# A hybrid transformer layer in float32: other feed-forward parts, a block-product end, and buffers in another order

## The chip, the cores and the metric

The kernel runs on one core of a Trainium2 chip. Five engines work side by side, each through its own queue in order: TensorE (PE; its weight loads are PEld), VectorE (DVE), ScalarE (ACT), GpSimd (POOL) and SyncE (SP), which issues the transfers between the chip's main memory (HBM) and the on-chip memory (SBUF). [...] The metric is the device time of one execution in microseconds (us); lower is better.

## The reference

One layer (`DEPTH` is 1) over 256 tokens of width 2048, all in float32. The mixer has 16 heads in two groups; then comes a feed-forward with a causal convolution of width 3 over the tokens.

```python
D_MODEL = 2048; SEQ = 256
D_FF = ((8 * D_MODEL // 3 + 255) // 256) * 256        # 5632 = 44 tiles of 128

def hybrid_mixer(h, ...):
    proj = h @ w_in_l
    ...                                               # q, k, v of both groups, forget gates
    out_a = forgetting_attention(qa, ka, va, c)       # softmax with a cumulative log-forget bias
    out_b = stick_breaking_attention(qb, kb, vb)      # sigmoid breaks, strictly causal
    merged = concat([rms_norm(out_a, g_fox), rms_norm(out_b, g_sb)])
    return merged @ w_out_l

def conv_ffn(h, w_up_l, conv_w_l, conv_b_l, w_down_l):
    u = h @ w_up_l                                    # 2048 -> 2 x 5632
    u = causal_depthwise_conv(u, conv_w_l) + conv_b_l
    gate, val = jnp.split(u, 2, axis=-1)
    return (jax.nn.silu(gate) * val) @ w_down_l       # 5632 -> 2048

x = x + hybrid_mixer(rms_norm(x, attn_norm), ...)
x = x + conv_ffn(rms_norm(x, ffn_norm), ...)
```

## The kernel before

**Precision.** Every matrix product is made of three: both operands are split into a high part, rounded to the format in which TensorE is fast, and a low part, the rest. `split` does that for weights: ScalarE casts the raw tile to `w_hi` (L208), VectorE subtracts to `w_lo` (L209). The products are hi x hi, hi x lo and lo x hi. Each weight tile is 1 MB, loaded by `load` (L201) through SyncE into `w_raw`, then split, then used.

**Mixer.** `token_major` (L237 to L239) and `feature_major` (L252, L257) stream weight tiles against `hT`, the normalised tokens transposed. The attention heads are generators that are stepped between the products. The last products are with `w_out`; each of their four column blocks adds to `x` (L561), sums squares for the second norm (L163, tile `junk`) and is transposed into `hT` (L148, L153, L154). All buffers of this stage lie in pools that are closed at its end: `wpool` with 3 raw, 2 hi and 2 lo tiles, `at` with what lives long (among it `oT`, the heads' outputs), `tmp` with what lives short (among it `raw` and `junk`).

**Feed-forward.** Its weights have a pool `wff` of their own (4 raw, 3 hi, 3 lo, one `w_sum`), placed where the mixer's pools were. The 44 feature tiles are taken in parts (`FFN_PARTS`): 8, 8, 8, 8, 8 and 4. Within a part, each two tiles need a `gate` and a `val` up-projection, each a `feature_major` of two halves (one weight tile, 32 matmuls each). `convolved` takes the sum out of PSUM (tile `t`, L268, L269), scales it (`up`, L597) and convolves (L601, L606). Then `silu(gate) * val` (L765, L766) is split into `g` (L768, L769). `combinations` makes from the tiles of two pairs the token sums `s` (L645 to L651), which the block products need; its `t` tiles come from the same two buffers as those of the evacuation.

**Down-projection, one part behind.** The part's down-projection runs beside the next part's up-projection: `step`, called after each half, adds `pace` to a counter, and each 16 releases one step of the generators in `behind`. For parts of 8 tiles these are `down_in_seven`: two by two blocks (two blocks of 4 feature tiles, two token tiles, 1024 columns) done in seven block products instead of eight, by sums of weights and sums of tokens. Each product is 12 matmuls of 512 columns (L675) against one split tile; between them VectorE sums weights into `w_sum` (L698, L706, L726) or a raw tile (L717) and adds the bank to `x` (L682). Its order before: w11 with `g`, then four products with token sums `s`, then w21 with `g` (the last two pairs), and a last one with `g`. Three PSUM banks are used in turn, `bank_a`, `bank_b` and `bank_c`. `down_plain` does the same columns with eight tiles' worth of plain products (L747 to L749), 24 matmuls a step. The last part of 4 tiles has its own loop of `token_major` (L783 on) with an add (L788) and the stores (L790) after each 512 columns.

**Order.** The framework lays instructions on the engines' queues by priority, which is the order of the program except where `tc.high_priority(offset=...)` moves instructions ahead: weight loads and splits by `AHEAD` = 200 instructions, PSUM evacuations by twice that. A tile that reuses a buffer waits until the last reader of the old tile is done, and a pool that is placed over closed pools waits for them.

Of the kernel before, what the change touches and what calls it, by code (L numbers as in the profile page):

```python
# [38 lines left out]
WINDOW = 2  # L39
FFN_PARTS = [(f, min(f + 8, NFT)) for f in range(0, NFT, 8)]  # L40


@with_exitstack
def hybrid_layer(
# [114 lines left out]
    def sums_of_squares(ss, c):  # L159

        for t in range(NT):
            junk = tmp.tile([P, 512], F32, name="junk", tag="raw", bufs=4)
            act.activation(junk, xt[t][:, c * 512 : (c + 1) * 512], AF.Square, accum_out=ss[:, t, c : c + 1])  # L163
# [34 lines left out]
    def load(src, into=None):  # L198
        raw = into if into is not None else wpool.tile([P, 2048], F32, name="w_raw", tag="w_raw")
        a, b = src.shape[1:]  # L200
        nc.sync.dma_start(raw[:, : a * b].rearrange("p (a b) -> p a b", a=a), src)  # L201
        return raw

    def split(raw, a, b):
        hi = wpool.tile([P, 2048], F32R, name="w_hi", tag="w_hi", bufs=n_split)
        lo = wpool.tile([P, 2048], F32R, name="w_lo", tag="w_lo", bufs=n_split)
        n = a * b
        act.copy(hi[:, :n], raw[:, :n])  # L208
# [63 lines left out]
    with ExitStack() as actx:  # L272
        n_split = 2
        wpool = actx.enter_context(tc.tile_pool(name="wpool", bufs=3))
        at = actx.enter_context(tc.tile_pool(name="at", bufs=1))
        pss = actx.enter_context(tc.tile_pool(name="pss", bufs=2, space=bass.MemoryType.PSUM))
        tmp = actx.enter_context(tc.tile_pool(name="tmp", bufs=2))

        def project(c0, cols, **kw):
# [12 lines left out]
        def fox_rows(acc, dst, g):  # L292

            rows = []
            for t in range(NT):
                raw = tmp.tile([P, 512], F32, name="raw", tag="raw", bufs=4)
                scaled(raw, acc[:, t, :], t)
                rows.append(raw)
            for t in range(NT):
                raw = rows[t]  # L300
                r3 = raw.rearrange("p (h d) -> p h d", h=4)
                sq = tmp.tile([P, 512], F32, name="sq", tag="raw", bufs=4)
                dve.tensor_tensor(sq, raw, raw, op=ALU.mult)
# [15 lines left out]
        ssq = [at.tile([P, S], F32, name=f"ssq{i}") for i in range(2)]  # L319

# [28 lines left out]
        acc_q0 = project(0, 512, pieces=(2,) * 8, before=opening)  # L349
        masks = tmp.tile([P, 4 * P], F32, name="masks", tag="raw", bufs=4)  # L350
        load_parameters(masks)
# [303 lines left out]

    def down_in_seven(f0, pairs, sums, c0):
# [4 lines left out]
        x11, x12 = xt[0][:, c0 : c0 + 512], xt[0][:, c0 + 512 : c0 + 1024]  # L661
        x21, x22 = xt[1][:, c0 : c0 + 512], xt[1][:, c0 + 512 : c0 + 1024]

        def of_pairs(h, t):
            return lambda a, part, j: pairs[2 * h + a][:, part, j, t * P : (t + 1) * P]
# [13 lines left out]

        def add(to, bank, op=ALU.add):  # L680
# [8 lines left out]
        with ahead():  # L689
            w = wpool.tile([P, 2048], F32, name="w_sum", tag="w_sum", bufs=1)  # L690
# [9 lines left out]
        product(bank_b, True, of_sums(0), parts)  # L700
        add(x22, bank_b)
        yield
# [4 lines left out]
        product(bank_b, False, of_sums(2), parts)  # L707
        add(x12, bank_b)
# [4 lines left out]
        add(x12, bank_a, ALU.subtract)  # L713
        yield
# [4 lines left out]
        product(bank_a, False, of_sums(3), parts)  # L719
        add(x22, bank_a, ALU.subtract)  # L720
# [12 lines left out]
        add(x21, bank_a)  # L733
        yield

    def down_plain(f0, pairs, c0, cols):
        for c in range(c0, c0 + cols, 512):
            acc = [psf.tile([P, 512], F32, name="bank_a", tag="a") for _ in range(NT)]
            for k0 in range(0, 2 * len(pairs), 4):
# [10 lines left out]
                if last:  # L750
                    for t in range(NT):
                        xs = xt[t][:, c : c + 512]
                        dve.tensor_tensor(xs, acc[t], xs, op=ALU.add)
                yield

    for n_part, (f_lo, f_hi) in enumerate(FFN_PARTS):
        pairs, gates, sums = [], [], []
        n_behind = 0
        last_part = n_part == len(FFN_PARTS) - 1

        pace = (11 if last_part else 14) * 8 // (f_hi - f_lo)
        for f in range(f_lo, f_hi, 2):
# [11 lines left out]
        while behind:  # L774
            n_behind, pace = 16, 0
            step()
        if not last_part:
            behind.append(down_in_seven(f_lo, pairs, sums, 0))
            if f_hi + 8 > NFT:
                behind.append(down_plain(f_lo, pairs, 1024, 1024))  # L780
            else:
                behind.append(down_in_seven(f_lo, pairs, sums, 1024))
    for c in range(4):  # L783
        acc = token_major(
            lambda k: pairs[k // 2][:, :, k % 2, :], wd, f_lo, f_hi - f_lo, 512 * c, 512
        )
        xs = x2[:, :, c * 512 : (c + 1) * 512]
        dve.tensor_tensor(xs, acc, xs, op=ALU.add)  # L788
        for t in range(NT):
            nc.sync.dma_start(of[t * P : (t + 1) * P, c * 512 : (c + 1) * 512], xs[:, t, :])  # L790

# [56 lines left out]
```

## Time and profile before

| | |
|---|---|
| time, median of 3 | 1193.19 us (1192.18 to 1194.01) |
| the profiled execution | 1194.88 us |
| its span, first to last instruction | 1193.1 us |
| TensorE busy | 1144.6 us, 96% of the span |
| TensorE weight load | 970.8 us, 81% |
| VectorE busy | 904.9 us, 76% |
| ScalarE busy | 616.8 us, 52% |
| granted TensorE clock, mean | 0.974 |
| moved from and to HBM | 229 MB, 192 GB/s over the span |
| mixer, to its last matmul | 0 to 413 us |
| feed-forward | 413 to 1193 us |

The busy share is an average over stages. In the mixer VectorE and ScalarE are about half busy; in the feed-forward parts VectorE is nine tenths busy beside a TensorE that is nearly always busy. A busy TensorE can still be slow: the granted clock says at which share of full speed it ran. "Idle before, <-" names what an engine waited for last.

### The profile page before, as it was taken

To read this page: it belongs to the slowest core of one execution; us is meant where nothing else is said; L and a number is where in the kernel's file an instruction comes from. 1 tells how busy PE (TensorE), PEld (TensorE's weight loads), DVE (VectorE), ACT (ScalarE), POOL (GpSimd) and SP (SyncE) were. 2 spreads that over 40 slices of the span, in tenths; PEclk is the share of its full clock that TensorE was granted. 3 is DMA by queue.
4 is the path that set the end of the run, shared out by engine and by line. 5 is a ranking of instruction groups with operands and counts; after the bars stand their busy time and mean duration, and the time that the engine had idled before them with its cause. 6 is when DMAs were issued, how large, how long until landed. Compare 5 with 4: busy or idle time off the path is not lost.

```text
span 1193.1 us, 14521 instructions
## 1 busy us (share of the span) xinstructions
PE 1144.6 (96%) x5894; PEld 970.8 (81%) x5894; DVE 904.9 (76%) x978; ACT 616.8 (52%) x667; POOL 0.2 (0%) x4
## 2 busy tenths in 40 slices
PE   7999999999999899997999899998999979998998
PEld 6998888888888778886888678886888868886886
DVE  4646656565565666788899989998899989999864
ACT  4644454445654545554656445554655545554641
POOL 0000000000000000000000000000000000000000
PEclk9999999999999989998999989998999989998999
DMA  6665555555445296554768556774767657665651
GB/s 224 212 218 182 173 175 173 156 166 167 151 142 176 72 324 201 184 177 151 237 213 256 187 190 212 235 238 161 242 204 234 205 174 231 219 220 176 212 176 71
DMA packets 172046, 230.27 MB, mean 193 GB/s; under 512 B 4025, under 2 KB 117835, under 8 KB 171979
## 3 DMA queue, kind: packets, MB, share of 16 engines
q1 hardware_dynamic: 171978, 229.35, 59.3%
q8 instruction: 46, 0.75, 0.3%
q14 instruction: 22, 0.17, 0.0%
HBM read 227.23 MB, written 2.10 MB: 192 GB/s over the span
## 4 chain that ended last, share of the span: by engine, by line
PE 90%; DVE 4%; ACT 3%; DMA 2%; issue 1%; SPq 0%; ACTq 0%; DVEq 0%
PE pu L252 31%; PE pu L257 15%; PE bank_a L675 8%; PE acc L238 8%; PE acc L237 8%; PE acc L239 8%; PE bank_b L675 5%; ACT w_hi L208 2%; DVE w_lo L209 2%; PE bank_c L675 2%; PE bank_a L747 1%; PE bank_a L749 1%; PE bank_a L748 1%; PE ps_x L148 1%; DMA x<-in_x_dram 0%
## 5 line engine op out<-in xcount | busy, mean ns | idle before, releaser
L209 DVE TENSOR_TENSOR w_lo<-w_raw,w_hi 128x2048 fp32r<-128x2048 f32 (+2 forms) x195 | 429.7, 2203 | 184.0 <-ACT w_hi L208 183.5
L208 ACT CAST w_hi<-w_raw 128x2048 fp32r<-128x2048 f32 (+2 forms) x195 | 358.6, 1840 | 339.0 <-PE pu L252 116.8
L252 PE MATMUL pu<-hT,w_hi 128*128 128x512 f32 x1664 | 527.5, 398 | 0.4 <-ACT w_hi L208 0.4
L257 PEld LDWEIGHTS pu<-hT,w_lo 128*128 128x128 f32 x1664 | 314.8, 189 | 76.0 <-DVE w_lo L209 1.8
L257 PE MATMUL pu<-hT,w_lo 128*128 128x256 f32 x1664 | 330.2, 280 | 1.1 <-DVE w_lo L209 1.1
L252 PEld LDWEIGHTS pu<-hT,w_hi 128*128 128x128 f32 x1664 | 261.0, 190 | 6.9 <-ACT w_hi L208 0.7
L237 PE MATMUL acc<-w_hi,hT 128*128 128x512 f32 (+1 forms) x320 | 120.4, 376 | 0.0
L238 PE MATMUL acc<-w_lo,hT 128*128 128x512 f32 (+1 forms) x320 | 119.2, 373 | 0.6 <-DVE w_lo L209 0.6
L239 PE MATMUL acc<-w_hi,hT 128*128 128x512 f32 (+1 forms) x320 | 119.0, 372 | 0.0
L208 ACT CAST w_hi<-w_sum 128x2048 fp32r<-128x2048 f32 x36 | 68.7, 1909 | 68.7 <-PE pu L252 46.5
L209 DVE TENSOR_TENSOR w_lo<-w_sum,w_hi 128x2048 fp32r<-128x2048 f32 x36 | 82.3, 2287 | 14.0 <-ACT w_hi L208 14.0
L675 PE MATMUL bank_b<-w_hi,s 128*128 128x512 f32 x144 | 58.7, 466 | 17.2 <-ACT s L650 10.3
L238 PEld LDWEIGHTS acc<-w_lo,hT 128*128 128x128 f32 x320 | 60.6, 189 | 9.7 <-DVE w_lo L209 1.5
L239 PEld LDWEIGHTS acc<-w_hi,hT 128*128 128x128 f32 x320 | 60.6, 189 | 8.8
L237 PEld LDWEIGHTS acc<-w_hi,hT 128*128 128x128 f32 x320 | 60.8, 190 | 8.1
L675 PE MATMUL bank_a<-w_hi,s 128*128 128x512 f32 x144 | 51.6, 418 | 9.8 <-ACT w_hi L208 9.8
L675 PEld LDWEIGHTS bank_b<-w_hi,s 128*128 128x128 f32 x144 | 31.9, 226 | 27.9 <-ACT s L650 11.8
L675 PE MATMUL bank_a<-w_hi,g 128*128 128x512 f32 x144 | 48.1, 395 | 0.0
L675 PEld LDWEIGHTS bank_a<-w_hi,s 128*128 128x128 f32 x144 | 28.4, 197 | 18.7 <-ACT w_hi L208 12.8
L606 DVE SCALAR_TENSOR_TENSOR gate<-up,ccol,gate 128x256 f32<-128x256 f32 x88 | 38.6, 481 | 3.6 <-ACT gate L601 3.4
L606 DVE SCALAR_TENSOR_TENSOR val<-up,ccol,val 128x256 f32<-128x256 f32 x88 | 38.2, 480 | 0.9 <-ACT val L601 0.7
L237 PE MATMUL acc<-w_hi,oT 128*128 128x512 f32 x96 | 38.1, 397 | 0.0
(186 smaller groups left out, 1182.3 us busy)
## 6 DMA issues: line engine op xcount, KB each, us to landing
w_raw<-in_w_up_dram SPq DMA_DIRECT2D x88, 1024.0 KB, 5.2
w_raw<-in_w_down_dram SPq DMA_DIRECT2D x53, 1024.0 KB, 5.1
w_raw<-in_w_in_dram SPq DMA_DIRECT2D x36, 1024.0 KB, 5.1
w_raw<-in_w_out_dram SPq DMA_DIRECT2D x16, 1024.0 KB, 5.1
w_sum<-in_w_down_dram SPq DMA_DIRECT2D x9, 1024.0 KB, 5.2
w_raw<-in_w_in_dram SPq DMA_DIRECT2D x12, 688.0 KB, 4.0
w_raw<-in_w_in_dram SPq DMA_DIRECT2D x8, 512.0 KB, 3.9
out_dram<-x SPq DMA_DIRECT2D x8, 256.0 KB, 2.5
```

Of the source, the lines that this page charges most:

```text
L148: nc.tensor.transpose(ps[:, j, t * P : (t + 1) * P], xt[t][:, (k + j) * P : (k + j + 1) * P], ident)
L208: act.copy(hi[:, :n], raw[:, :n])
L209: dve.tensor_tensor(lo[:, :n], raw[:, :n], f32(hi[:, :n]), op=ALU.subtract)
L237: nc.tensor.matmul(o, lhi, hi[:, i, :], start=first, stop=False)
L238: nc.tensor.matmul(o, lhi, lo[:, i, :], start=False, stop=False)
L239: nc.tensor.matmul(o, llo, hi[:, i, :], start=False, stop=last)
L252: nc.tensor.matmul(acc[:, j, :], hi[:, i, j * P : (j + 1) * P], hT[:, k].rearrange("p a b -> p (a b)"), start=k == 0, stop=False,)
L257: nc.tensor.matmul(acc[:, j, S:], lo[:, i, j * P : (j + 1) * P], hT[:, k, 0, :], start=False, stop=k == KT - 1,)
L606: dve.scalar_tensor_tensor(a[:, j, :], u[:, j, w : w + S], ccol[:, w, f : f + 1], a[:, j, :], op0=ALU.mult, op1=ALU.add,)
L675: nc.tensor.matmul(bank, lhs(a, l, j), r[:, i, :], start=first and i + n == 0, stop=i == 3 and n == 2, skip_group_check=not first,)
L747: nc.tensor.matmul(acc[t], g[:, 0, ts], hi[:, i, :], start=first, stop=False)
L748: nc.tensor.matmul(acc[t], g[:, 0, ts], lo[:, i, :], start=False, stop=False)
```

## The change

- The feed-forward's parts become 4, 8, 8, 8, 8, 8 tiles. The first part's down-projection is plain (`down_plain` over all 2048 columns, four steps, released at a pace of 4), those of the following four parts are two `down_in_seven` each.
- The last part has 8 tiles and its down-projection runs after all up-projections: the first 1024 columns by `down_in_seven` (called `heavy`), the other 1024 by `down_plain` (`light`), their steps interleaved by hand. Each block of 512 columns is stored as soon as its last addition is made.
- In `down_in_seven` the product of w21 with the last two pairs' `g` moves from sixth to second place, so that the products with token sums begin with the third. w21 is loaded a second time for the sum of the last product.
- Pools: raw, hi and lo weight tiles and `w_sum` get pools of their own in both stages, in another order; the mixer's `raw`, `junk`, `sq`, `masks`, `oT` and `ssq` go to a pool `late` behind the others. Counts of buffers stay as they were.

```diff
-FFN_PARTS = [(f, min(f + 8, NFT)) for f in range(0, NFT, 8)]
+FFN_PARTS = [(max(f, 0), f + 8) for f in range(-4, NFT - 4, 8)]
...
     with ExitStack() as actx:
-        n_split = 2
-        wpool = actx.enter_context(tc.tile_pool(name="wpool", bufs=3))
         at = actx.enter_context(tc.tile_pool(name="at", bufs=1))
...
         tmp = actx.enter_context(tc.tile_pool(name="tmp", bufs=2))
+        wraw = actx.enter_context(tc.tile_pool(name="wraw", bufs=3))
+        whi = actx.enter_context(tc.tile_pool(name="whi", bufs=2))
+        wlo = actx.enter_context(tc.tile_pool(name="wlo", bufs=2))
+        late = actx.enter_context(tc.tile_pool(name="late", bufs=1))
...
-        oT = [at.tile([P, 2, S], F32R, name=f"oT{h}") for h in range(2 * NH - 4)]
+        oT = [late.tile([P, 2, S], F32R, name=f"oT{h}") for h in range(2 * NH - 4)]
...
-    n_split = 3
-    wpool = ctx.enter_context(tc.tile_pool(name="wff", bufs=4))
+    wlo = ctx.enter_context(tc.tile_pool(name="wlo2", bufs=3))
+    whi = ctx.enter_context(tc.tile_pool(name="whi2", bufs=3))
+    wraw = ctx.enter_context(tc.tile_pool(name="wraw2", bufs=4))
+    wsum = ctx.enter_context(tc.tile_pool(name="wsum", bufs=1))
...
+        adds = {}
+
+        def add(t, half, bank, op=ALU.add):
+            c = c0 + 512 * half
+            to = xt[t][:, c : c + 512]
             with tc.high_priority(offset=2 * AHEAD):
                 dve.tensor_tensor(to, to, bank, op=op)
+            adds[t, half] = adds.get((t, half), 0) + 1
+            if final and adds[t, half] == (1 if (t, half) == (1, 0) else 2):
+                store(t, c)
...
         product(bank_a, True, of_pairs(0, 0), parts)
-        add(x11, bank_a)
+        add(0, 0, bank_a)
+        yield
+        bank_c = psb.tile([P, 512], F32, name="bank_c", tag="t")
+        with ahead():
+            parts = split(load(w21), 4, 512)
+        product(bank_c, True, of_pairs(1, 0), parts)
+        add(0, 0, bank_c)
         yield
...
-        bank_c = psb.tile([P, 512], F32, name="bank_c", tag="t")
-        with ahead():
-            b21 = load(w21)
-            parts = split(b21, 4, 512)
-            dve.tensor_tensor(w, w, b21, op=ALU.add)
-        product(bank_c, True, of_pairs(1, 0), parts)
-        add(x11, bank_c)
-        yield
         with ahead():
+            dve.tensor_tensor(w, w, load(w21), op=ALU.add)
             parts = split(w, 4, 512)
         product(bank_a, False, of_pairs(1, 1), parts)
-        add(x21, bank_a)
+        add(1, 0, bank_a)
...
-    def down_plain(f0, pairs, c0, cols):
+    def down_plain(f0, pairs, c0, cols, final=False):
         for c in range(c0, c0 + cols, 512):
-            acc = [psf.tile([P, 512], F32, name="bank_a", tag="a") for _ in range(NT)]
+            if final:
+                acc = psa.tile([P, NT, 512], F32, name="acc", tag="acc")
+                acc = [acc[:, t, :] for t in range(NT)]
+            else:
+                acc = [psf.tile([P, 512], F32, name="bank_a", tag="a") for _ in range(NT)]
...
-        pace = (11 if last_part else 14) * 8 // (f_hi - f_lo)
+        pace = 4 if n_part == 1 else 14
...
-        if not last_part:
-            behind.append(down_in_seven(f_lo, pairs, sums, 0))
-            if f_hi + 8 > NFT:
-                behind.append(down_plain(f_lo, pairs, 1024, 1024))
-            else:
-                behind.append(down_in_seven(f_lo, pairs, sums, 1024))
-    for c in range(4):
-        acc = token_major(
...
+        if n_part == 0:
+            behind.append(down_plain(f_lo, pairs, 0, D))
+        elif not last_part:
+            behind += [down_in_seven(f_lo, pairs, sums, c) for c in (0, 1024)]
+    heavy = down_in_seven(f_lo, pairs, sums, 0, final=True)
+    light = down_plain(f_lo, pairs, 1024, 1024, final=True)
+    for g in (light, heavy, heavy, light, heavy, heavy, light, heavy, heavy, heavy, light):
+        next(g)
```

More of the change, by code (lines that the diff above doesn't have):

```diff
@@ L161, in sums_of_squares @@
         for t in range(NT):
[L162 removed]
+            junk = late.tile([P, 512], F32, name="junk", tag="raw", bufs=4)
             act.activation(junk, xt[t][:, c * 512 : (c + 1) * 512], AF.Square, accum_out=ss[:, t, c : c + 1])
@@ L198, in load @@
     def load(src, into=None):
-        raw = into if into is not None else wpool.tile([P, 2048], F32, name="w_raw", tag="w_raw")
+        raw = into if into is not None else wraw.tile([P, 2048], F32, name="w_raw", tag="w_raw")
         a, b = src.shape[1:]
@@ L295, in fox_rows @@
             for t in range(NT):
-                raw = tmp.tile([P, 512], F32, name="raw", tag="raw", bufs=4)
+                raw = late.tile([P, 512], F32, name="raw", tag="raw", bufs=4)
                 scaled(raw, acc[:, t, :], t)
@@ L301, in fox_rows @@
                 r3 = raw.rearrange("p (h d) -> p h d", h=4)
-                sq = tmp.tile([P, 512], F32, name="sq", tag="raw", bufs=4)
+                sq = late.tile([P, 512], F32, name="sq", tag="raw", bufs=4)
                 dve.tensor_tensor(sq, raw, raw, op=ALU.mult)
@@ L349, in hybrid_layer @@
         acc_q0 = project(0, 512, pieces=(2,) * 8, before=opening)
-        masks = tmp.tile([P, 4 * P], F32, name="masks", tag="raw", bufs=4)
+        masks = late.tile([P, 4 * P], F32, name="masks", tag="raw", bufs=4)
         load_parameters(masks)
@@ L700, in down_in_seven @@
         product(bank_b, True, of_sums(0), parts)
-        add(x22, bank_b)
+        add(1, 1, bank_b)
         yield
@@ L707, in down_in_seven @@
         product(bank_b, False, of_sums(2), parts)
-        add(x12, bank_b)
+        add(0, 1, bank_b)
         yield
@@ L712, in down_in_seven @@
         product(bank_a, False, of_sums(1), parts)
-        add(x12, bank_a, ALU.subtract)
+        add(0, 1, bank_a, ALU.subtract)
         yield
```

27 lines of the change are left out of this document (11 added, 16 removed).

## The prediction

> **What bounds the kernel now.** I read the page first. TensorE is busy 96% of the span and carries 90% of the chain that ended last, so time is lost only where it waits or runs slowly. Next the chain of waits in order of time, for the length of undisturbed work:
>
> ```profile
> 568.48 2.80 PE bank_a L675 x12
> 576.86 2.80 PE bank_c L675 x12
> 585.24 2.80 PE bank_a L675 x12
> ```
>
> A block product takes 2.80 us and the next starts 8.38 us after it, so the half up-projection between takes 5.58. A part of 8 tiles has 16 halves and 14 products: 16 x 5.58 + 14 x 2.80 = 128.5 us. Busy time by stretches, cut at the same point of successive parts (columns: length, then PE, weight load, DVE, ACT, POOL busy, granted clock, DMA share, GB/s):
>
> ```profile
> 412.00:436.00 24.00, 18.41 (x85) 14.66 (x84) 14.04 (x22) 11.20 (x15) 0.00 (x0) 0.79 0.99 309
> 560.33:699.27 138.94, 132.95 (x682) 111.97 (x681) 126.00 (x121) 76.06 (x67) 0.00 (x0) 0.96 0.65 212
> 699.27:837.12 137.85, 132.35 (x682) 111.41 (x681) 125.97 (x121) 76.03 (x67) 0.00 (x0) 0.96 0.65 214
> 837.12:975.91 138.79, 132.80 (x681) 111.90 (x681) 125.98 (x121) 76.04 (x67) 0.00 (x0) 0.96 0.65 212
> 1088.00:1106.00 18.00, 12.36 (x35) 8.55 (x35) 16.04 (x18) 8.54 (x8) 0.00 (x0) 0.72 0.36 117
> ```
>
> Each full part takes 138 to 139 us: 10.5, 9.4 and 10.3 us more than its work, with a clock of 0.96 instead of 1.00. TensorE's timeline shows where, in every part alike (in brackets: idle before, and what ended it):
>
> ```profile
> 681.11 0.50 PE L675 MATMUL bank_b<-w_hi,s 128*128 128x512 f32 x1 [2.32 <-ACT s L650]
> ...
> 683.51 1.22 PE L675 MATMUL bank_b<-w_hi,s 128*128 128x512 f32 x2 [1.68 <-DVE s L651]
> ...
> 687.58 0.79 PE L675 MATMUL bank_a<-w_hi,s 128*128 128x512 f32 x1 [1.99 <-ACT w_hi L208]
> ```
>
> The second product of a part wants the token sums `s` of the last pair, which VectorE has not made: its `val` convolution (L606) runs at 672.43 to 676.3, the sums (L651) at 682.77. Idle time is 6.0 us; the rest is the clock, 0.53 over 683 to 694. The same happens at 540, 817 and 955, and worse at 1088, where 30 matmuls (7.0 us) take 1088.79 to 1106.02, 10.2 us too long. The fifth place is the start of the feed-forward, in the waits of SyncE's queue and its timeline:
>
> ```profile
> SPq L201 <- PE acc L239: 7.5, 1, 7.5
> ```
>
> ```profile
> 413.15 9.63 SPq L201 DMA_DIRECT2D w_raw<-in_w_up_dram  x5
> ```
>
> The first `w_up` load is issued at 413.15, after the last attention matmul (413.12). Load 5.0, cast 1.9 and subtraction 2.3 us then stand in a row; TensorE needs until 435.73 for 8 transposes, 4 small matmuls and two halves, worth 12.8 us: 9.8 lost.
>
> Lost in all: 9.8 + (10 at 540, taken like the next three) + 30.2 + 10.2 = 60.2 us. The floor of this order of engines is 1193.1 - 60.2 = 1132.9 us of span.
>
> **Part by part.** *Parts 4, 8, 8, 8, 8, 8.* TensorE's count does not change: 88 halves, 9 x 7 products and 8 plain steps of 24 matmuls before and after; nor do VectorE's 195 + 36 splits or ScalarE's. The work moves. Before, the last part had 4 tiles and 11 down steps of the part before it, which is the pile-up at 1088; after, the short part comes first with nothing behind it, the second has 4 plain steps, and the crowded place is gone (10.2). What is exposed instead is the end: 7 products and 4 plain steps, 7 x 2.80 + 4 x 5.60 = 42.0 us of TensorE with no up-projection beside them, where 22.4 us stood. That is already in the floor; what is not is VectorE in those 42 us. Back to back it spends 2.20 us on a split or a weight sum (519.94, 522.14, 524.34 in its timeline) and 0.61 on a 512-column add: 11 splits + 4 sums = 33.0, 11 adds 6.7, the last pair's chain (two evacuations, convolutions, product, `g`, sums) about 8, its `gate` convolution 1.6: 49 us, less two splits made ahead (4.4): 45, against 42. The adds now also stand between consecutive products on one bank (bank_b twice, bank_a three times, no half between): three waits of about 1.2 us, 0.2 for the hand-over and 0.68 for the add and its release. The second `heavy` step needs the last pair's `g` about 12.6 us after the last half ends; VectorE has 15 us of work before it, so 3 more are late. From 3 (VectorE alone) to 16 (all these and a stretch of slow clock); I take 10, the sum of 3, 3.6 and 3. Final adds and stores are as before: 5.6 us from last matmul to span's end.
>
> *Token sums late.* The second product becomes w21 with the last pairs' own `g` (L769 at 677.74, before the 678.78 at which TensorE stopped), the sums come one step (8.38 us) later. Before that second product one weight sum less (2.2 us) stands ahead of the convolution on VectorE, so `s` is ready near 682 where it would be wanted near 680. What is late next: the PSUM evacuation `t` (L268), which shares its two buffers with the combinations and so waits for `s`, in the list of waits:
>
> ```profile
> ACT t L268 <- DVE s L651: 7.7, 4, 1.9
> ```
>
> Its add ends at 686.87; TensorE would want that bank at 682.9, and moved ahead by 2.2 to 4.4 us it is 0 to 2 us late. VectorE is busy 126.0 us of a part that shall take 128.5, so there is cover, but little. Bounds for one boundary: 0.5 and 10 (unchanged); I take 2.5, the upper end of those waits with half a chance of slow clock. Four boundaries: 10 instead of 40.
>
> *The reload.* w21 is loaded twice: 9 more loads of 1 MB in SyncE's queue, ahead of `w_up` loads in places. DMA share 0.65 with 28 loads in 138.5 us becomes 0.75 with 30 in 128.5; the queue moved 350 GB/s at 418 to 426. Four raw buffers turn over in 4 x 128.5 / 28 = 18 us, and a load needs 5.2 + 1.9 + 2.3. So nothing, covered by that slack (and no gain, since nothing is taken away); if it is gone, see the fourth rival.
>
> *Buffers reordered.* The row buffers and `oT` go to a pool of their own behind the weights, so that the new raw tiles lie over `tmp` and the old raw tiles, and the new hi and lo tiles over `at` and `tmp`. By the tile sizes, `at` + `tmp` are 57,536 bytes a partition and old raw tiles end at 82,112; the new raw pool ends at 81,920, short of the old w_hi. The last old raw tile is read until 405.64 (L209), so loads can go 7.5 us earlier, land from 410.7 on, be cast by 412.6 and subtracted by 415. TensorE then waits some 2 us where it lost 9.8: I leave 3 (1 to 9.8). Moving `raw` and `w_hi` pools within the attention phase changes no count of buffers: nothing.
>
> Sum: 1132.9 + 3 + 10 + 10 = 1155.9 of span. Time is 1.8 over span in the profiled run (1194.88), and that run is 1.7 above the median, so 1156 against 1193.19.
>
> **The clock.** Each of the long stalls is followed by about 10 us at 0.50 (0.53 over 417:428 and 683:694, 0.51 over 1093:1103, back at 1.00 at 554 and 694): some 4 us on top of 6. The rows say 10 us, and I go by them. [...]
>
> **Rivals.**
> 1. *VectorE becomes the bound.* It idles 12.9 us a part now, mostly waiting for ScalarE's cast. If it idles as long however the steps are ordered, a part stays at 138.5: 1132.9 + 3 + 40 + 10 = 1186. For: 126.0 of 128.5. Against: the stall after part 0, which had no products behind it and a VectorE with slack, is as long as those after full parts, so it is a matter of order.
> 2. *The end runs at half clock.* A 2.80 us product between waits of 2 us for VectorE brings the slow clock again and again: 52 us hold five stretches of 10, at 4 us each 20 more: 1176. For: gaps of 2.32 and 1.68 did it at 683. Against: plain steps of 5.60 lie between. [...]
> 3. *The loads do not go earlier* (the new tiles still touch something alive): 7 more, 1163.
> 4. *Slower: the reloaded w21 is late.* Seventh product of every block step: load, sum, cast, subtract are 5.2 + 2.3 + 1.9 + 2.3 = 11.7 us in a row; if the load cannot run ahead of the step before (8.38), TensorE waits 3.3 each time and 4 go to the clock: 9 x 7.3 = 66, 1222. It decides from 4.1 us per block step. Against: ScalarE waited for raw `w_up` data 3 times, 4.7 us in all.
>
> **How the numbers follow.** Forecast 0.48, rival 1 0.20, rival 2 0.10, rival 3 0.10; slower (rival 4, or 1 and 2 together with the end at 20: 1206) 0.09; within 0.2%, which is about what can be told from no change here, 0.03. Faster is 0.88. The low end has 1, 4 x 0.5 and 3 left over: 1139. The high end reaches rival 1: 1186.
>
> **Right or wrong.** Right: `w_up` loads at 406, a clock of 1.00 at 417, no wait for `s` over 1 us at part boundaries, part periods near 131, VectorE over 95% busy in them, 50 to 54 us from the last half to the last matmul. Wrong: periods near 138 (rival 1), 0.5 clock through the end (2), loads still at 413 (3), waits for DMA in ScalarE's rows (4).

## The result and the profile after

The changed kernel takes 1178.78 us (median of 4, 1178.28 to 1179.02) against 1193.6: 0.9877 of the time, 95% interval 0.986 to 0.9894. Faster by 1.2%, with an interval clear of no change: the forecast direction, but 15 us where 37 were forecast. The profiled span is 1177.2 us, at a mean granted clock of 0.987 instead of 0.974. From the page of the changed kernel:

```profile
span 1177.2 us, 14561 instructions
PE 1135.4 (96%) x5894; PEld 963.1 (82%) x5894; DVE 904.7 (77%) x982; ACT 617.0 (52%) x667; POOL 0.2 (0%) x4
```

As many matmuls as before, 9 us less of TensorE time. Busy time by stretches of the changed kernel (columns as before the change): the start of the feed-forward, two full parts cut at the same point of each, the rest of the last part's up-projection, and the end, from the last block product of the part before to the last matmul.

```profile
415.64:432.75 17.11, 15.74 (x97) 13.50 (x95) 13.77 (x24) 10.94 (x15) 0.00 (x0) 1.00 1.11 341
721.58:858.86 137.28, 132.21 (x681) 111.54 (x681) 125.97 (x121) 76.22 (x67) 0.00 (x0) 0.98 0.70 230
858.86:995.77 136.91, 131.84 (x681) 111.20 (x681) 125.91 (x121) 76.21 (x67) 0.00 (x0) 0.98 0.70 230
1113.75:1172.55 58.80, 46.43 (x181) 35.20 (x180) 46.76 (x44) 23.58 (x19) 0.00 (x0) 0.91 0.38 131
```

The start now runs at a clock of 1.00 (0.79 before). The full parts still take 137 us for 128.5 of work. The end takes 58.8 for 42.0 of work. What TensorE waited for, in all (last columns: us, times, longest):

```profile
PE bank_c L681 <- ACT g L787: 9.0, 1, 9.0
PE pu L252 <- DVE t L269: 6.9, 3, 2.3
PE bank_a L681 <- ACT w_hi L208: 6.0, 3, 2.0
...
PE bank_b L681 <- DVE s L656: 2.4, 3, 0.8
```

The first row is the end, the other three are the three boundaries after a full part: 1.99, 0.78 and 2.30 us of idle time at each, 15.3 in all. Behind them stand four stretches of half clock (3.41 us from 707.15, 741.29 and 843.69, 6.83 from 877.82), 17.1 us, which cost about half of that, 8.5. Behind the third boundary's gaps the clock stayed at 1.00. So the three cost about 24 us. The waits for sums (10.3 and 6.9 us before) are down to 2.4; in their place an up-projection half (`pu`, L252) waits for the addition that empties its PSUM bank (`t`, L269). The sum of the prediction against this trace:

| term, us over the floor of 1132.9 | forecast | measured |
|---|---|---|
| start of the feed-forward | 3 | 1.4 |
| first boundary, behind the short part | 2.5 | 0 |
| three boundaries behind full parts | 7.5 | about 24 |
| end, 42.0 us of work | 10 | 16.8 |
| mixer | 0 | 2.5 |
| last matmul to end of span | 0 | -1.0 |
| span | 1155.9 | 1177.2 |

The measured terms add up to 1176.6; 0.6 us are not accounted for.

Two theories for the boundaries: (1) the two buffers that the evacuations share with the combinations; (2) VectorE has too little room, rival 1. For the end: (1) the last pair's chain stands too late in VectorE's queue; (2) the block products ask more of VectorE and of the loads than 42 us hold.

### The profile page after: what moved, and what is told of

It reads as the page before. It is cut to its first block, busy times and chain, and to the rows that moved or that the text cites. A ratio compares the mean times of both kernels' runs of the same rounds, so it can differ in the third digit from the quotient of the medians.

```text
span 1177.2 us, 14561 instructions
## 1 busy us (share of the span) xinstructions
PE 1135.4 (96%) x5894; PEld 963.1 (82%) x5894; DVE 904.7 (77%) x982; ACT 617.0 (52%) x667; POOL 0.2 (0%) x4
## 4 chain that ended last, share of the span: by engine, by line
PE 83%; DVE 8%; DMA 3%; issue 2%; ACT 2%; SPq 0%; DVEq 0%; ACTq 0%
PE pu L252 30%; PE pu L257 15%; PE acc L238 7%; PE acc L237 7%; PE acc L239 7%; PE bank_a L681 7%; DVE w_lo L209 4%; PE bank_b L681 3%; ACT w_hi L208 2%; DMA w_raw<-in_w_down_dram 2%; PE bank_c L681 1%; DVE val L611 1%; PE bank_a L764 1%; PE bank_a L766 1%; PE bank_a L765 1%
## 5 line engine op out<-in xcount | busy, mean ns | idle before, releaser
L252 PE MATMUL pu<-hT,w_hi 128*128 128x512 f32 x1664 | 528.4, 399 | 6.9 <-DVE t L269 6.9
L257 PEld LDWEIGHTS pu<-hT,w_lo 128*128 128x128 f32 x1664 | 315.7, 190 | 75.9 <-DVE w_lo L209 1.8
L257 PE MATMUL pu<-hT,w_lo 128*128 128x256 f32 x1664 | 331.0, 280 | 1.4 <-DVE w_lo L209 1.4
L252 PEld LDWEIGHTS pu<-hT,w_hi 128*128 128x128 f32 x1664 | 260.9, 191 | 13.3 <-issue 8.1
L681 PE MATMUL bank_b<-w_hi,s 128*128 128x512 f32 x144 | 48.7, 398 | 3.0 <-DVE s L656 2.4
L681 PE MATMUL bank_a<-w_hi,s 128*128 128x512 f32 x144 | 48.2, 395 | 0.9 <-DVE x L692 0.9
L237 PE MATMUL acc<-w_hi,oT 128*128 128x512 f32 x96 | 38.0, 396 | 0.0
L681 PEld LDWEIGHTS bank_a<-w_hi,g 128*128 128x128 f32 x144 | 27.0, 187 | 13.0 <-ACT w_hi L208 7.3
L239 PE MATMUL acc<-w_hi,oT 128*128 128x512 f32 x96 | 37.5, 390 | 0.0
```

The source lines that it names most:

```text
L237: nc.tensor.matmul(o, lhi, hi[:, i, :], start=first, stop=False)
L239: nc.tensor.matmul(o, llo, hi[:, i, :], start=False, stop=last)
L252: nc.tensor.matmul(acc[:, j, :], hi[:, i, j * P : (j + 1) * P], hT[:, k].rearrange("p a b -> p (a b)"), start=k == 0, stop=False,)
L257: nc.tensor.matmul(acc[:, j, S:], lo[:, i, j * P : (j + 1) * P], hT[:, k, 0, :], start=False, stop=k == KT - 1,)
L681: nc.tensor.matmul(bank, lhs(a, l, j), r[:, i, :], start=first and i + n == 0, stop=i == 3 and n == 2, skip_group_check=not first,)
```

## The experiments

All times are medians, with the ratio to the kernel before and its 95% interval.

**1. The pools alone**, on the kernel before.

```diff
-        wpool = actx.enter_context(tc.tile_pool(name="wpool", bufs=3))
+        wraw = actx.enter_context(tc.tile_pool(name="wraw", bufs=3))
...
+        late = actx.enter_context(tc.tile_pool(name="late", bufs=1))
```

> The kernel before with the new pools alone. If the parts of the change add up: the first w_up load near 408 instead of 413, 8 us less between the last attention matmul and the second half (1.4 lost where 9.8 were), but the mixer 2.5 us longer, as in the changed kernel, since its matmuls there start every 233 ns instead of 227 with the same order on TensorE: about 1188. If the longer mixer came from something else in the change, the mixer ends near 413 and the time is near 1185.

1187.85 us, 0.9956 (0.994 to 0.9973): the gain at the start as expected, less a mixer that is some 2 us longer.

**2. The order alone** (token sums late, w21 loaded twice), on the kernel before.

```diff
+        product(bank_c, True, of_pairs(1, 0), parts)   # second
...
-        product(bank_c, True, of_pairs(1, 0), parts)   # sixth
```

> The kernel before with the new order of the seven products alone (w21 second, loaded twice). If the order is what shortens the part boundaries: the first boundary, after a part with nothing behind it, loses almost nothing instead of 10 us, the other three about 8.5 each instead of 10: about 1179. If it was the lighter second part that freed the first boundary, all four lose 8.5: about 1187. The pile-up in the last part stays in both (10).

1160.94 us, 0.9734 (0.9719 to 0.9748). Better than the whole change, and 18 us better than either expectation: a boundary behind a full part keeps one gap of 1.99 us, no wait for `s` and none for `t`. The row of the waits that is left holds three of these gaps and one in the last part:

```profile
PE bank_a L675 <- ACT w_hi L208: 7.2, 4, 2.0
```

**3. The parts and the new end alone**, with the old order and pools.

```diff
-FFN_PARTS = [(f, min(f + 8, NFT)) for f in range(0, NFT, 8)]
+FFN_PARTS = [(max(f, 0), f + 8) for f in range(-4, NFT - 4, 8)]
...
+    heavy = down_in_seven(f_lo, pairs, sums, 0, final=True)
+    light = down_plain(f_lo, pairs, 1024, 1024, final=True)
```

> The kernel before with parts of 4, 8, 8, 8, 8, 8 and the new end, but old pools and the old order of products. If the parts add up: the pile-up goes (10 less), the end loses 17 or more, the four boundaries lose 10 each as before: 1193 - 10 + 17 = 1200, up to 1210 since the old order wants the token sums second at the end too. If the gain of the change came from the parts: under 1190.

1185.19 us, 0.9931 (0.9916 to 0.9946), 15 us better than the sum of the parts said and under the 1190 of the other branch: alone, the parts gain. The first boundary, behind the short part, is free; the later ones keep their stalls; in the end TensorE waits 1.3, 1.4 and 7.1 us.

**4. The combinations in place**, on the changed kernel: their intermediates are written over `val` and `gate`, which nobody reads any more, instead of into two buffers `t2` that the evacuations use too.

```diff
-        t = [ff.tile([P, 2, 2, P], F32, name="t2", tag="t2") for _ in range(2)]
+        t = [val.rearrange("p q (j c) -> p q j c", j=2),
+             g1.rearrange("p j (q c) -> p q j c", q=2)]
```

> The changed kernel with the combinations' intermediate tiles written over the dead val and gate tiles instead of taking the two buffers of the PSUM evacuation. Same instructions on every engine. Theory 1, the shared buffers hold up the evacuation and through it TensorE: the waits of pu for t (2.3 us, three times) go, and the product placed ahead of its turn (2.0 us, three times) with them, with the slow clock after them: up to 8 us a boundary, 24 in all, 1155; at least 12, 1167. Theory 2, VectorE's 126 us of work in a part cannot be done in less than 137: parts stay at 137, 1179.

1153.75 us, 0.967 (0.9656 to 0.9685): 25 us off the changed kernel. What is left, in the waits of TensorE and in the busy time of a stretch of 131 us that is a little longer than one full part:

```profile
PE bank_c L684 <- ACT g L790: 7.6, 1, 7.6
...
PE pu L257 <- DVE w_lo L209: 1.8, 4, 1.2
PE acc L768 <- DVE w_lo L209: 1.5, 2, 1.0
...
692.00:823.00 131.00, 130.81 (x690) 110.95 (x689) 128.02 (x126) 76.80 (x67) 0.00 (x0) 1.00 0.75 248
```

All waits at boundaries are gone, the one for `w_hi` too, and a part of 680 matmuls takes 129.0 us from one point to the same point of the next, where the changed kernel took 137. VectorE is busy 128.0 of these 131 us (98%) and TensorE 130.8 at full clock: the amount of VectorE's work did not cause the stalls; who held the two buffers did. Theory 1 holds, rival 1 falls.

**5. The last pair's chain first**, on the changed kernel: in the last part its convolutions, `g` and sums go at high priority.

```diff
+    def soon(f):
+        if f == NFT - 2:
+            return tc.high_priority(offset=2 * AHEAD)
+        return ExitStack()
...
-            act.activation(gate, gate, AF.Silu)
+            with soon(f):
+                act.activation(gate, gate, AF.Silu)
...
```

> The changed kernel with one priority altered: in the last pair of the last part, the convolution, product, g and token sums are placed ahead of the weight work of the end. Theory 1, the 9.0 us wait of TensorE for g at the end arises because VectorE stands at a weight sum of a later product (L737, waiting for its transfer) with the val convolution queued behind it: that wait falls to under 3 us and the slow clock after it goes, 9 to 13 less than 1178.8, 1166 to 1170. Theory 2, VectorE simply has too much to do at the end: the wait comes back at the weight tiles, and the time stays within 3 of 1178.8. The part boundaries are as in the changed kernel in both.

1175.4 us, 0.985 (0.9828 to 0.9872). Only 3.4 us: just outside the 3 of theory 2, far from the 9 to 13 of theory 1. TensorE no longer waits for `g`, but now for weight tiles and additions in the end (lines of its waits; the first holds the three boundaries' 6.0 as well):

```profile
PE bank_a L690 <- ACT w_hi L208: 7.0, 4, 2.0
...
PE acc L774 <- DVE w_lo L209: 2.5, 2, 1.5
...
PE bank_a L690 <- DVE w_lo L209: 1.8, 1, 1.8
...
PE bank_a L690 <- DVE x L701: 1.1, 1, 1.1
```

**6. Both, 4 and 5.**

> Both edits on the changed kernel: sums in place (1153.8 by itself) and the end's chain first. By theory 1 the two are independent: 1153.8 less 9 to 13, 1141 to 1145. By theory 2, within 3 of 1153.8.

1153.79 us, 0.9669 (0.9652 to 0.9685): no better than 4 alone. The wait for `g` (7.6 us in run 4) is gone, and waits for weight tiles and additions stand in its place, among them these:

```profile
PE bank_b L693 <- DVE w_lo L209: 2.4, 1, 2.4
...
PE bank_b L693 <- DVE x L704: 1.9, 1, 1.9
```

The wait only moves. Theory 2 for the end.

**7. The combinations in place on the kernel before.**

> The kernel before with the combinations in place, and nothing of the change. If the shared evacuation buffers alone made the stalls at the part boundaries: the 10 us at each of four boundaries go, 1153. If the late token sums are a wait of their own (TensorE's first gap at each boundary ended with the cast of s): the first two gaps (2.3 and 1.7) and the slow clock stay, only the third (2.0) goes: 1180 to 1187.

1176.93 us, 0.9866 (0.9851 to 0.9881): the shared buffers cost the kernel before 16 us too. That is neither of the two expected times: less than all four boundaries are worth, more than the third gap. TensorE keeps a wait of up to 2.7 us for `w_hi` at the start of an up-projection half (L252) at the later boundaries.

**8. Late sums, pools and in place, with the old parts 8, 8, 8, 8, 8, 4 and the old end.**

> Everything of the change but its parts and end (8, 8, 8, 8, 8, 4 and the old last loop), with sums in place. If the new parts gain once the boundaries are free: this is slower than 1153.8. If the parts are what the change loses by: the order alone gave 1160.9, with three waits of 2.0 us and slow clock (3.7 each, 11) and a late start of the feed-forward (8.4, less 2.3 for the mixer) to take off, 1144, and less where the pile-up in the last part (4.3 and 1.2) eases.

1149.22 us, 0.9637 (0.9622 to 0.9651): better than 4 by 4.5 us. With free boundaries the new parts and their end, taken together, lose; run 11 tells the two apart.

**9 and 10. Which part gives the late sums' gain back?** The changed kernel with the old parts and end, and the changed kernel with the old pools.

> The changed kernel with the old parts of 8, 8, 8, 8, 8, 4 tiles and the old end: late token sums and reordered pools only. Late sums alone gave 1160.9 us and the pools alone took 5.2 us off the kernel before. Theory A, the new parts (with the end that hangs on them) give back what the late sums won: the two add up, 1155 to 1158 us, with at most one gap of 2 us at each boundary after a full part. Theory B, the reordered pools give it back, because the first weight splits of a part then come at another time: the stalls on the evacuation t are back as in the changed kernel, 6 to 8 us at each boundary, 1172 to 1180 us.

> The changed kernel with the pools as before: late token sums and new parts. Theory A, the new parts give back what the late sums won: stalls on the evacuation at the three boundaries after full parts and the long end, about 1178.8 plus the 5 us that the pools are worth, 1181 to 1186 us. Theory B, the pools give it back: the boundaries have one gap of 2 us each, and only the end stays long, 1164 to 1172 us.

1154.94 us, 0.968 (0.9665 to 0.9694), and 1183.65, 0.9916 (0.9889 to 0.9944; its four executions spread from 1178.97 to 1187.05). Theory A in both. With the late sums alone as base, the pools bring 6.0 us (1160.94 to 1154.94) and the new parts cost 22.7 (1160.94 to 1183.65); on the changed pools they cost 23.8 (1154.94 to 1178.78), though on the kernel before they brought 8. The traces show where it arises. ScalarE's timeline around the evacuations of the last pair's `gate` and `val`, first the changed kernel, then that with the old parts:

```profile
702.68 0.57 ACT L268 COPY t<-pu 128x512 f32<-128x512 f32 x1
703.15 0.62 ACT L655 CAST s<-t 128x512 fp32r<-128x512 f32 x1
703.86 1.90 ACT L208 CAST w_hi<-w_sum 128x2048 fp32r<-128x2048 f32 x1
706.93 0.59 ACT L268 COPY t<-pu 128x512 f32<-128x512 f32 x1 [1.18 <-DVE s L656]
```

```profile
765.27 1.05 ACT L268 COPY t<-pu 128x512 f32<-128x512 f32 x2
766.45 1.90 ACT L208 CAST w_hi<-w_sum 128x2048 fp32r<-128x2048 f32 x1
```

With the old parts the two evacuations run one behind the other. With the new ones a cast of the first combinations' sums (L655) stands between them, and the second evacuation, 4.25 us after the first, waits for its buffer until VectorE's `s` (L656) is done. On VectorE the scaling of `val` that follows (`up`, L602) then comes at 717.79, 12.0 us after the gap of TensorE that ends at 705.81, instead of 3.8 after the one that ends at 768.40; the last pair's sums come at 737.49 instead of 792.82, 31.7 us after that gap instead of 24.4, and TensorE wants them 28 to 30 after it. Why the framework orders the same instructions differently when a short part has gone ahead was not settled.

**11. A plain end**, on 4: the whole last down-projection by plain steps, so the last part makes no combinations.

```diff
-    heavy = down_in_seven(f_lo, pairs, sums, 0, final=True)
-    light = down_plain(f_lo, pairs, 1024, 1024, final=True)
-    for g in (light, heavy, heavy, light, ...):
-        next(g)
+    for _ in down_plain(f_lo, pairs, 0, D, final=True):
+        pass
...
-            if len(pairs) > 2:
+            if len(pairs) > 2 and not last_part:
```

> The kernel with the combinations in place (1153.75 us), but the whole last down-projection in plain steps, so the last part needs no combinations and no block products: TensorE has 192 products of 233 ns, 44.8 us, after the last g instead of 180, 42.0, and VectorE has eight weight splits, eight additions and no weight sums. Theory 1, the end is bound by what the block products ask of VectorE and of the loads: the gaps of the end (11 us, with the slow clock behind them 15 to 16) go down to 2 or 3, against 2.8 us more of matmuls: 1141 to 1145 us. Theory 2, the end is late because the last pair's g is late whatever follows: the first product of the last g still waits 7 us, and 2.8 us are added: 1152 to 1157 us.

1141.22 us, 0.9566 (0.9552 to 0.958): 12.5 us less with 12 more matmuls. From the end of the last up-projection to the last matmul:

```profile
1086.84:1134.44 47.60, 47.60 (x204) 37.80 (x203) 26.06 (x26) 15.72 (x12) 0.00 (x0) 1.00 0.37 122
```

TensorE works all of the 47.6 us, at full clock, beside a VectorE busy 26. Theory 1 as it was put for this run: the end was bound by what the block products ask for. This kernel is also 8.0 us faster than run 8 with the old parts and the old end: with free boundaries and a plain end the new parts gain, so what lost against run 8 was the end by block products.

**12. The plain end on the changed kernel**, combinations elsewhere not in place.

> The changed kernel with the last down-projection in plain steps only, and no combinations in the last part; combinations elsewhere not in place. Theory 1, the block products cost the end by themselves what they cost with the combinations in place (12.5 us): 1165 to 1168 us, with the three boundaries as in the changed kernel. Theory 2, the gain of a plain end needs the combinations in place: 1173 us or more.

1167.1 us, 0.9781 (0.9763 to 0.9798): 11.7 less than the changed kernel, so the end's cost stands by itself. Boundaries and end are two separate terms: 25.0 and 12.5 (runs 4 and 11) make up most of what can be won back.

**13 to 15. The mixer's 2.5 us.** In the changed kernel, and in 1, the mixer's products of 512 columns with `hT` start every 233 ns, in the kernel before every 227, with the same instructions on TensorE in the same order; only the byte addresses differ. Three kernels with other stackings of the pools: 8 with the mixer's split weights and the `g` tiles low in a partition; 11 with the same; 11 with the feed-forward's weights high, below `g` and `s`.

```diff
+    g2p = ctx.enter_context(tc.tile_pool(name="g2p", bufs=8))
+    whi = ctx.enter_context(tc.tile_pool(name="whi2", bufs=3))
     wlo = ctx.enter_context(tc.tile_pool(name="wlo2", bufs=3))
-    whi = ctx.enter_context(tc.tile_pool(name="whi2", bufs=3))
```

> Late sums, reordered pools, combinations in place and the old parts (1149.2 us), with the pools stacked so that the mixer's split weights lie low (from byte 73,312 of a partition instead of 155,424) and the feed-forward g tiles too. Nothing is computed otherwise or in another order. Theory 1, where the operands lie decides how fast products follow one another: the mixer's products with hT are back at 227 ns, and its end comes 2 to 2.5 us earlier, 1146 to 1147.5 us; if the feed-forward products with g also go down from 233 ns, each ns is worth about 1.5 us more. Theory 2, the spacing hangs on something else (what runs beside them): 233 ns as before, 1148.5 to 1150 us.

> Plain end, combinations in place (1141.2 us), with the pools stacked so that the mixer's split weights and the feed-forward g tiles lie low in a partition (from byte 73,312). If where the operands lie decides the spacing, the 640 products of the mixer with hT and the 750 or so with g follow at 227 ns instead of 233: 3.9 and 4.5 us of products, of which old parts with the same layout got 4.1 together: 1135 to 1138 us. If not, 1140.5 to 1142.

> The same instructions with another stacking: in the mixer the split weights lie low again, as before the change (hT products at 227 ns); in the feed-forward the split weights lie high (bytes 130,720 to 179,872) and g and s above them. Theory 1, operands of one product are fastest when weights and g are both high, and the products with hT streaming against weights that lie high follow at 229.5 ns, as the mixer's pu products do in the changed kernel, instead of 233: 1664 x 3.4 ns = 5.7 us, with 6 ns for each of some 750 products with g, 4.5 us, and 2.5 us in the mixer: 1128 to 1132 us. Theory 2, the feed-forward products keep 233 ns wherever their weights lie: only the mixer's 2.5 us, 1138 to 1140 us, or more if the fourth load of weights starts later.

1145.12 us, 0.9594 (0.9578 to 0.961): 4.1 less than 8. 1136.46, 0.9527 (0.9511 to 0.9542): 4.8 less than 11. 1144.47, 0.9588 (0.9571 to 0.9605): 3.3 more than 11, although its products with `g` and `s` stand at 227 to 228 ns, because the first `w_up` tiles lie over living ones again and the stalls at the start are back (3.0, 3.4 and 1.1 us). The chain of waits, twelve products to a line (start, length), in the changed kernel, in the low and in the high stacking:

```profile
586.50 2.80 PE bank_a L681 x12
...
603.26 2.80 PE bank_b L681 x12
```

```profile
583.13 2.73 PE bank_a L685 x12
...
599.72 2.80 PE bank_b L685 x12
```

```profile
594.05 2.73 PE bank_a L686 x12
...
610.63 2.73 PE bank_b L686 x12
```

`bank_a` takes `g` here, `bank_b` takes `s`. In the low stacking, where `g` has a pool of its own below the weights, only the products with `g` are shorter; in the high one, those with `s` too. By start times the feed-forward products with `g` follow every 227.4 ns instead of 233.6, the mixer's with `w_lo` and `hT` every 227.2 instead of 233.3. Addresses decide the spacing.

**16 to 18. Is it the address modulo 128?** That products are fast where both operands have the same address modulo 128 was the guess after run 15. Empty tiles of 64 bytes ahead of the mixer's weights and of `g` and `s`; the same with 128 bytes; and 64 bytes ahead of the feed-forward's weights as well.

```diff
+        actx.enter_context(tc.tile_pool(name="pad1", bufs=1)).tile([P, 16], F32, name="pad1")
         wraw = actx.enter_context(tc.tile_pool(name="wraw", bufs=3))
...
+    ctx.enter_context(tc.tile_pool(name="pad2", bufs=1)).tile([P, 16], F32, name="pad2")
     ff = ctx.enter_context(tc.tile_pool(name="ff", bufs=2))
```

> Plain end, combinations in place (1141.2 us), and an empty tile of 64 bytes ahead of the mixer's weight pools and another ahead of the pool with g and s: these lie 64 bytes further on, nothing else changes. Theory 1, products are at 227 ns where stationary and moving operand have the same address modulo 128: now hT, oT, g, s and all split weights have 96. Mixer 2.5 us shorter, and 950 feed-forward products with g and s at 227 instead of 233, 5.5 us: 1132.5 to 1134.5 us. Theory 2, distance or the half of a partition decides: nothing moves, 1140.5 to 1142.

> The control: the same empty tiles with 128 bytes. Theory 1: spacings as without them, 233 ns, 1140.5 to 1142 us. If any shift of these pools helps, as fast as with 64 bytes.

> 64 bytes ahead of the mixer's weights as in the first; in the feed-forward 64 bytes ahead of the weights and 64 more ahead of g and s, so that weights, g and s all have 32 modulo 128 and hT, which streams against the weights as stationary operand, has 96. Theory 1: products with g and s at 227 ns, as with 64 bytes; the 512-column products of the up-projection with w_hi as stationary operand, 233 ns so far, go to 230 or 231 as where the weights lay high, 1664 x 2 to 3 ns, while those of 256 columns take 1 ns more: 1130 to 1134 us. Theory 2: 1140.5 to 1142.

1139.09 us, 0.9549 (0.9534 to 0.9563); 1138.09, 0.9535 (0.9519 to 0.9551); 1135.48, 0.9523 (0.9508 to 0.9537). Both theories fall: the shift of 64 bytes ends between their times, and the control, which should have changed nothing, is 3.1 us faster than 11. In all three TensorE carries out the same instructions as in 11, in the same order. The control moved as much as the shift of 64. In the chain, 64 bytes and then 128:

```profile
583.47 2.80 PE bank_a L686 x12
```

```profile
583.12 2.76 PE bank_a L686 x12
```

The mixer's `w_lo` products with `hT` are at 227.3 and 228.1 ns, the feed-forward's with `g` and `s` at 231 to 234 and 228 to 231, by kind of product: for the most part neither 227 nor 233. Some shift helps, by no rule that these runs show. The last of them and the low stacking of 11 are the fastest kernels of the study, equal within their intervals: 0.9523 and 0.9527, 43 us better than the change.

## Why the prediction was right in direction and wrong in size

- *Transition, right.* The first `w_up` load goes out at 408.06 (SyncE's queue below), not at 413.15; 406 was forecast. The clock over 415.64 to 432.75 is 1.00, and 1.4 us are lost where 3 were left.

```profile
408.06 5.05 SPq L201 DMA_DIRECT2D w_raw<-in_w_up_dram  x4
```

- *The crowded last part, right.* The stall at 1088 is gone.
- *Token sums late: the mechanism right, the term mis-sized.* The wait for `s` went as described (17.2 us to 2.4). The step that failed is the 2.5 us a boundary, taken from "moved ahead by 2.2 to 4.4 us it is 0 to 2 us late" for the evacuation behind the combinations' buffers. The three boundaries behind full parts cost about 24 us where the three had 7.5. The evacuation itself was 2.30 us late at each, little more than the step allowed. What it left out is two things. One is the third gap of before (1.99 us, at 687.58): there one matmul of the next block product stands ahead of its turn and waits for its cast weights. The prediction counted it among the stalls of the late sums and gave no reason why it should go; it stayed, 6.0 us in all:

```profile
705.81 0.50 PE L681 MATMUL bank_a<-w_hi,g 128*128 128x512 f32 x1 [1.99 <-ACT w_hi L208]
```

  The other is the slow clock, which the step gave half a chance and which came four times (8.5 us). The wait on the shared buffers was seen in the list of waits and priced by its length before (1.9 us at most). Run 4 shows that this one sharing carries all three gaps; how it comes to put one matmul ahead of its turn was not shown.
- *The sum of the parts.* The prediction had each edit keep its price beside the others. On the old parts its price for the late sums was about right (30 us forecast, run 2 brought 31.8). By their ratios the order brought these 31.8 us alone and the parts 8.2 (runs 2 and 3), but together, on the old pools, 10.0 (run 10; 6.7 to 13.2 by its interval): the parts moved the combinations into the evacuations' way. No step of the prediction allowed for that.
- *The end: 16.8 instead of 10*, 0.8 above its bounds of 3 to 16. The term "3 more are late" for `g` was 9.05 us; beside it stood four waits of 0.6 to 1.0, one of them at an addition, instead of the three of 1.2 at additions, and one stretch of slow clock of 10.24 us. That VectorE's 45 us do not fit well into 42 was the right reason: run 11 takes the work away and the stall goes.
- *"Changes no count of buffers: nothing."* The mixer lost 2.5 us without a new wait, and runs 13 to 18 put this down to the addresses.
- *Rivals.* The parts' period is near 138 as rival 1 said, and its cause is not VectorE's amount (run 4). Rival 4 did not come: run 2 reloads w21 and gains 32 us. Rival 2 did not: one stretch of slow clock in the end, not five. Rival 3 did not.
- *The floor was good at this spacing of products.* 1132.9, with 2.8 for the plain end, 2.5 for the mixer, 1.4 at the start and 1.0 less behind the last matmul, is 1138.6; run 11 has a span of 1139.3. It is no floor of the hardware: run 18, with the same instructions and other addresses, has 1133.1.

**The clock.** The prediction went by stretches of 10 us, from rows of before. In the changed kernel the half clock behind the boundary gaps is shorter (windows of it, columns as above; the clock is the third number from the end):

```profile
703.80:707.15 3.35, 1.36 (x8) 1.17 (x8) 3.35 (x5) 2.11 (x2) 0.00 (x0) 1.00 0.70 191
707.15:710.56 3.41, 3.41 (x13) 2.92 (x12) 3.36 (x4) 0.59 (x2) 0.00 (x0) 0.50 0.70 272
710.56:714.00 3.44, 3.44 (x22) 3.00 (x21) 3.26 (x4) 1.62 (x3) 0.00 (x0) 1.00 0.08 8
```

One gap of 1.99 us is followed by 3.41 us at 0.50; the other slow stretches ahead of the last matmul in these traces last 3.41, 6.83, 10.24 or 13.65 us, whole multiples. The stretches of 10 us that the prediction went by are three times 3.41. One of the kernel before:

```profile
683.55:693.79 10.24, 8.25 (x20) 6.08 (x21) 7.31 (x7) 3.01 (x3) 0.00 (x0) 0.50 0.64 205
```

Cut into three windows of 3.41 us, it has TensorE idle for 1.37, 0.62 and 0.00 us: the gap that ends at 687.58 reaches into the first two of them, and the third is dense.

## What to carry to other kernels

When an edit moves a chain of work earlier, list who shares buffers with each tile of that chain, and price the next wait by how long its holder may keep the buffer once the order changes, not by how long the wait was before. Scratch tiles of a side computation do not belong in the buffers that empty PSUM; here dead tiles could take them, for 25 us. Measure the edits of a bundle singly and in pairs: this one held one edit worth 32 us, and another that gave back 23 of them.

## What the runs showed of the hardware

- A gap of 2 us in TensorE's work can be enough for 3.41 us of half clock, but is not always; in these traces it goes by where the gap lies. In each trace the slow stretches ahead of the last matmul begin whole multiples of 3.413 us apart (in the changed kernel at 707.15, 741.29, 843.69, 877.82 and 1133.82: 10, 30, 10 and 75 such windows from each to the next, 426.67 us for 125; in the kernel before at 417.31, 543.60, 683.55, 820.08, 960.03 and 1093.15: 37, 41, 40, 41 and 39), so they fit a fixed grid of that step. Here is run 9 cut at its grid; the second number is TensorE's busy time. The gap of 1.99 us that ends at 637.7 is split between two windows, and the clock stays at 1.00. The equal gap that ends at 899.1 lies within one window, and the next window is slow.

```profile
633.82:637.23 3.41, 1.88 (x9) 1.16 (x7) 2.94 (x3) 3.29 (x4) 0.00 (x0) 1.00 0.88 301
637.23:640.64 3.41, 2.96 (x16) 2.56 (x17) 3.41 (x4) 0.40 (x1) 0.00 (x0) 1.00 0.73 230
...
896.65:900.06 3.41, 1.42 (x8) 0.85 (x7) 3.41 (x4) 2.31 (x2) 0.00 (x0) 1.00 0.81 254
900.06:903.47 3.41, 3.41 (x13) 2.92 (x12) 3.41 (x4) 0.41 (x1) 0.00 (x0) 0.50 0.76 294
```

  Over the twenty traces, cut like this and past their first 10 us, a window at full speed in which TensorE sat idle for 1.88 us or more was always followed by half clock (in the changed kernel that of 874.41, with 1.88), and one with less than 1.7 us never (there that of 1014.35, with 1.58); in between both occurred. A slow window with at most 0.44 us of idle time ended its stretch (there that of 741.29, with 0.44), one with 0.59 or more did not (that of 686.96 before, with 0.62). So it is partly luck which of a kernel's 2 us gaps cost another 1.7 us, half of 3.41. This is worked out from the traces; no run was made to test it.
- The spacing of 512-column products depends on where the operands lie in SBUF: 227 or 233 ns, and values between, with identical instructions (2.7%). The mixer's `pu` products (weights `w_hi`, streamed `hT`) start every 233 ns in the kernel before and every 229 in the changed kernel (medians), while its token-major products with `hT` go from 227 to 233, so one layout can help one kind and hurt another. The rule is open: equality modulo 128 bytes is refuted by runs 16 and 17 (1139.09 and 1138.09 us, where it asked for 1132.5 to 1134.5 and 1140.5 to 1142). In the traces of before and after no two such products in a row start less than 224 ns apart.
- The split format is the faster one on TensorE. In the trace of before the next product starts 215 ns after one of 256 columns with plain float32 operands (`ps_o`, L457 and L523) and 116 ns after one with `w_lo` (L257), by medians.
